# A router's weights scaled by the norm's row, its logits laid out by tokens, and a gather cut in four

## The chip, the cores and the metric

One core of one Trainium2 chip runs the program. The metric is device time in microseconds of one execution; the time before is the median of three runs. The trace is of one further, profiled execution.

## The reference, cut to what matters

Two blocks follow each other (256 tokens, width 1024, fp32). The first (mixer, cross attention, convolutional FFN, conformer) and the attention of the second are not touched. The change lies at the end, between the second block's last projection and its mixture of experts:

```python
x = x + mix @ w_out                        # the last projection, 1024 -> 1024
h = rmsnorm(x, g_ffn)                      # x * rsqrt(mean(x*x) + eps) * g_ffn
g_logits = h @ w_group + b_group           # 4 groups
e_logits = h @ w_router + b_router         # 4 x 8 experts; the best group's 8 are kept
e_w, e_idx = top_k(softmax(e_logits of that group), 2)
for e in range(32):                        # D_EXPERT = 512
    a = silu(h @ w_e_gate[e]) * (h @ w_e_up[e])
    out = out + gates[:, e:e+1] * (a @ w_e_down[e])
# then x + out goes through the final rmsnorm
```

## The kernel before

Tokens lie in two tiles t of 128 rows, `self.x[:, t]`; the width is cut into eight chunks of 128 (KC). Instructions are written in program order and a scheduler orders them on each engine; every engine then takes its queue strictly in that order. `self.after` adds an ordering without a semaphore.

**Last projection** (`proj_rows`, L293). The weights come as four loads of 1 MB; each is split on ScalarE into a rounded high part and on VectorE into the remainder (`split`, L202: L219, L220) in tiles named `whl`, of which there are four. The first two loads go through `proj_tm`; for the last two, four quarters b = (t, h) of the result, h being half the width, are finished one after the other (L315 to L317). After quarter b, `Norm.a` (L60) adds it to x (L67), multiplies by the norm's row into `xn` (L73) and squares on ScalarE; `Norm.b` (L87) transposes a quarter of `xn` on TensorE and copies it to `xnT`; `then` issues the router's logits.

**Router** (`moe`, L1128). The logits come out as 36 x 128 (L1170: weights `wr` stationary, `xnT` moving), are copied to `lt` and transposed back to tokens by 36 (L1186). `stats` makes rstd. L1191 applies rstd and bias; `first_max` and its neighbours, all on VectorE, choose experts; a small product with a triangle of ones (L1213) counts positions. `wr` is loaded on ScalarE's queue (L1155).

**Experts.** 32 experts go in 8 groups q of four, 32 token slots each. `gather` (L1230) makes `xq` (the chosen tokens, by chunks) with a one-hot matrix; for q = 0 in two halves of four chunks, before any expert product. `stream` (L1322) multiplies one chunk with four experts' weights; G, U and Y are gate, up and down. `acc` holds x plus the experts' output: four products with the identity put x there (L1275).

**Weights.** The experts' 201 MB are loaded on SyncE's queue (SP) in fixed order into 22 places of 1 MB (`wl`, L1314): five double buffers of their own (`pairs`, L1297), then places that earlier stages give up, in this order: one of its own, the three of the ring (free when VectorE has split the load in them), the four `whl` tiles (free when the projection's last product has read them), the two row tiles, `mh`, `ml`, and last the tile of x itself (free when the four products of L1275 have read it). The 23rd load reuses the first double buffer, and so waits for the first two chunks of G. SP issues in order: a load whose place is not free holds back all behind it.

Of the kernel before, what the change touches and what calls it, by code (L numbers as in the profile page):

```python
# [43 lines left out]
class Norm:  # L44
# [57 lines left out]
    def stats(self, t):  # L102
# [3 lines left out]
        nc.vector.scalar_tensor_tensor(r, ss[:, t, 0:1], EPS, ss[:, t, 1:2], op0=OP.add, op1=OP.add)  # L106
# [30 lines left out]
    def rcb(self, n):  # L137
        return self.rc[:, None, :].to_broadcast([P, n, T])


class Kern:
# [134 lines left out]
    def proj_tm(self, acc, w, ah, al, first):  # L276


        nc = self.nc
        wh, wl = self.split(self.wload(w, 2, D))  # L280
        for k in range(2):
            for t in range(2):
                sh = ah(k)[:, t * P:(t + 1) * P]
                sl = al(k)[:, t * P:(t + 1) * P]
                st = first and k == 0
                for h in range(2):
                    nc.tensor.matmul(acc[t][h], sh, wh(k)[:, h * 512:(h + 1) * 512], start=st, stop=False)  # L287
                for h in range(2):
                    nc.tensor.matmul(acc[t][h], sh, wl(k)[:, h * 512:(h + 1) * 512], start=False, stop=False)  # L289
                for h in range(2):  # L290
                    nc.tensor.matmul(acc[t][h], sl, wh(k)[:, h * 512:(h + 1) * 512], start=False, stop=False)

    def proj_rows(self, acc, w, ah, al, order, first=True, last=True, norm=None):  # L293
# [11 lines left out]
        for b in range(4):  # L305
            t, h = divmod(b, 2)
            ts_ = slice(t * P, (t + 1) * P)
            hs = slice(h * 512, (h + 1) * 512)
            for j, (i, wh, wl) in enumerate(ws):
# [818 lines left out]
    def moe(self, ctx, m, r2a):  # L1128
# [32 lines left out]
        lt = m1([36, 2, P], F32, "lt")  # L1161
        lps = []

        def logits(i):

            t, h = divmod(i, 2)
            if h == 0:
                lps.append(self.psr([36, P], "lp"))
            for k in range(4 * h, 4 * h + 4):
# [5 lines left out]
        norm = Norm(self, a["g_ffn_2"], then=logits,  # L1175
                    tiles=(lambda: m1([P, D], F32, "xn", f"xn{next(nX)}"), lambda: m1([P, 4, T], F32, "xnT", f"xs{next(nT)}")))
        self.proj_rows(self.acc4(), lambda i: a["w_out_2"][i], *m, range(4), norm=norm)
# [6 lines left out]
        lp = self.psr([P, 2, 36], "lp")  # L1184
        for t in range(2):
            tr = nc.tensor.transpose(lp[:, t], lt[:, t], self.ident[:36, :36])  # L1186
        Lg = m1([P, 2, 4], F32, "Lg")
        Le = m1([P, 2, 32], F32, "Le")
        for o, c0, c1 in ((Le, 4, 36), (Lg, 0, 4)):
            for t in range(2):  # L1190
                nc.vector.scalar_tensor_tensor(o[:, t], lp[:, t, c0:c1], norm.r[:, t:t + 1], rb[:, c0:c1], op0=OP.mult, op1=OP.add)  # L1191
# [38 lines left out]
        def gather(q, h, sel):  # L1230

            if h == 0:
                xq[q] = m1([P, KC, P], F32, "xq", f"xs{q % 2}")
            ps = self.psr([P, 4, P], "ga")
            for c in range(4):
                cs = slice((4 * h + c) * P, (4 * h + c + 1) * P)
                for t in range(2):
                    nc.tensor.matmul(ps[:, c], xn[t][:, cs], sel[:, t], start=(t == 0), stop=(t == 1))
            nc.scalar.activation(xq[q][:, 4 * h:4 * h + 4], ps, AF.Copy)

        sel = select(0)
        for h in range(2):
            gather(0, h, sel)
# [28 lines left out]
        acc = self.acc4()  # L1272
        for t in range(2):
            for h in range(2):
                nc.tensor.matmul(acc[t][h], self.ident, self.x[:, t, h * 512:(h + 1) * 512], start=True, stop=False)  # L1275
# [46 lines left out]
        def stream(ps, lh, q, i, st, en):  # L1322
            w = wl(q, i)
            for e in range(4):
                nc.tensor.matmul(ps[32 * e:32 * e + 32], lh[:, 32 * e:32 * e + 32], w(e), start=st, stop=en)  # L1325
# [39 lines left out]
        for q in range(NQ):  # L1365
            x_ = xq[q]
            G = self.psr([P, 512], "G")
            for k in range(KC):
                stream(G, x_[:, k], q, k, k == 0, k == KC - 1)
# [6 lines left out]
            for k in range(KC):  # L1376
# [6 lines left out]
                if k in (4, 6) and q + 1 < NQ:  # L1383
                    gather(q + 1, k // 2 - 2, sel)
# [220 lines left out]
```

## Time and profile before

| | |
|---|---|
| time, median of 3 runs | 1627.76 us (1627.6 to 1628.19) |
| the profiled execution: time / span | 1636.39 us / 1634.5 us |
| busy: TensorE, VectorE, ScalarE | 91%, 52%, 41% of the span |
| DMA in the last third (the experts) | busy throughout, 421 to 425 GB/s |

Times in rows are microseconds from the span's start. A row of the timeline has start, duration, engine, line, operation, result and operands, and in brackets the engine's idle time before it and what ended that. TensorE makes two passes for one fp32 product, so its counts are twice those of the code. "q" behind an engine's name is its sequencer, which issues DMAs. The page's 40 slices show TensorE at 90% and more until slice 31, and the DMA engines full from slice 29 to the last but one.

### The profile page before, as it was taken

To read this page: it belongs to the slowest core of one execution; us is meant where nothing else is said; L and a number is where in the kernel's file an instruction comes from. 1 tells how busy PE (TensorE), PEld (TensorE's weight loads), DVE (VectorE), ACT (ScalarE), POOL (GpSimd) and SP (SyncE) were. 2 spreads that over 40 slices of the span, in tenths; PEclk is the share of its full clock that TensorE was granted. 3 is DMA by queue.
4 is the path that set the end of the run, shared out by engine and by line. 5 is a ranking of instruction groups with operands and counts; after the bars stand their busy time and mean duration, and the time that the engine had idled before them with its cause. 6 is when DMAs were issued, how large, how long until landed. Compare 5 with 4: busy or idle time off the path is not lost. (4 is left out here: it accounts for less than half of the span.)

```text
span 1634.5 us, 23715 instructions
## 1 busy us (share of the span) xinstructions
PE 1479.8 (91%) x9724; PEld 1133.7 (69%) x9724; DVE 851.4 (52%) x1553; ACT 663.8 (41%) x1061; POOL 82.4 (5%) x146
## 2 busy tenths in 40 slices
PE   8999999999989999999999999999998777676665
PEld 7988889999987688999988789789643222221211
DVE  7975677666899566776676765765500000000000
ACT  5764555545676454545554444454311000000001
POOL 0000000000057000100000000000000000000000
PEclk9999999999999999999999999999989878897887
DMA  7555445555643443655545236247999999999996
GB/s 265 193 188 180 143 167 191 185 192 187 218 151 104 161 162 104 219 181 194 186 162 206 99 128 213 78 153 286 356 381 423 421 423 425 424 422 421 425 423 268
DMA packets 52049, 396.58 MB, mean 243 GB/s; under 512 B 5952, under 2 KB 6112, under 8 KB 12256
## 3 DMA queue, kind: packets, MB, share of 16 engines
q1 hardware_dynamic: 49824, 388.80, 62.0%
q0 software_dynamic: 1680, 5.79, 1.1%
q8 instruction: 78, 1.28, 0.3%
q10 hardware_dynamic: 432, 0.41, 0.1%
q14 instruction: 35, 0.29, 0.0%
HBM read 393.94 MB, written 1.05 MB: 242 GB/s over the span
## 5 line engine op out<-in xcount | busy, mean ns | idle before, releaser
L220 DVE TENSOR_TENSOR whl<-w,whl 128x1024 fp32r<-128x1024 f32 (+1 forms) x344 | 404.8, 1184 | 207.3 <-ACT whl L219 206.7
L219 ACT ACTIVATE whl<-w 128x1024 fp32r<-128x1024 f32 (+1 forms) x344 | 345.7, 1020 | 296.3 <-PE pr L270 147.0
L267 PE MATMUL pr<-xth,whl 128*128 128x256 f32 x1472 | 370.0, 283 | 0.0
L268 PE MATMUL pr<-xtl,whl 128*128 128x256 f32 x1472 | 366.8, 281 | 0.0
L267 PEld LDWEIGHTS pr<-xth,whl 128*128 128x128 f32 x1472 | 277.3, 188 | 3.7 <-issue 2.8
L268 PEld LDWEIGHTS pr<-xtl,whl 128*128 128x128 f32 x1472 | 277.2, 188 | 1.9 <-issue 1.1
L270 PE MATMUL pr<-xth,whl 128*128 128x256 f32 x1472 | 236.7, 281 | 1.2 <-DVE whl L220 1.2
L270 PEld LDWEIGHTS pr<-xth,whl 128*128 128x128 f32 x1472 | 200.4, 188 | 2.9 <-issue 1.5
L1387 DVE TENSOR_TENSOR as<-sg,tp 128x512 f32<-128x512 f32 x8 | 5.5, 687 | 241.1 <-ACT GUs L1330 117.2
L1325 PE MATMUL U<-w,xq 128*32 128x512 f32 x512 | 81.0, 719 | 37.4 <-DMA w<-in_w_e_dram 37.3
L1325 PE MATMUL Y<-w,as 128*32 128x512 f32 x512 | 77.4, 737 | 30.4 <-DMA w<-in_w_e_dram 25.4
L1325 PE MATMUL G<-w,xq 128*32 128x512 f32 x512 | 74.0, 671 | 32.5 <-DMA w<-in_w_e_dram 32.5
L1349 DVE COPY sct<-st 128x256 f32<-128x256 f32 x8 | 3.4, 424 | 160.9 <-PE st L1347 160.9
L1325 PEld LDWEIGHTS Y<-w,as 128*32 128x32 f32 x512 | 16.0, 126 | 84.0 <-DMA w<-in_w_e_dram 39.0
L1325 PEld LDWEIGHTS U<-w,xq 128*32 128x32 f32 x512 | 14.4, 119 | 84.0 <-DMA w<-in_w_e_dram 49.7
L1325 PEld LDWEIGHTS G<-w,xq 128*32 128x32 f32 x512 | 13.4, 116 | 83.3 <-DMA w<-in_w_e_dram 62.4
L1395 ACT ACTIVATE ys<-Y,sm 128x512 f32<-128x512 f32 x16 | 11.0, 687 | 130.0 <-PE Y L1325 130.0
L1330 ACT ACTIVATE GUs<-G,sm 128x512 f32<-128x512 f32 x8 | 5.5, 687 | 129.1 <-PE G L1325 129.1
L827 DVE SCALAR_TENSOR_TENSOR cps<-gl,vec,cps 128x252 f32<-128x252 f32 (+18 forms) x144 | 56.1, 468 | 1.7 <-ACT cps L797 1.6
L819 POOL TENSOR_TENSOR cv<-cv,prod 128x470 f32<-128x470 f32 (+9 forms) x40 | 50.4, 1263 | 18.8 <-ACT prod L815 16.3
L287 PE MATMUL pa<-whl,ah 128*128 128x512 f32 x160 | 49.4, 390 | 0.0
L289 PE MATMUL pa<-whl,ah 128*128 128x512 f32 x160 | 49.4, 390 | 0.0
(438 smaller groups left out, 2318.7 us busy)
## 6 DMA issues: line engine op xcount, KB each, us to landing
w<-in_w_e_dram SPq DMA_DIRECT2D x94, 1024.0 KB, 22.5
w<-in_w_e_dram SPq DMA_DIRECT2D x45, 2048.0 KB, 22.3
w<-in_f_w_up_dram SPq DMA_DIRECT2D x48, 1024.0 KB, 4.8
w<-in_w_in_dram SPq DMA_DIRECT2D x25, 1024.0 KB, 4.8
w<-in_f_w_down_dram SPq DMA_DIRECT2D x24, 1024.0 KB, 4.9
w<-in_c_w_pw_dram SPq DMA_DIRECT2D x12, 1024.0 KB, 4.9
w<-in_ab_w_in_dram SPq DMA_DIRECT2D x9, 1024.0 KB, 5.0
w<-in_xa_wk_dram SPq DMA_DIRECT2D x8, 1024.0 KB, 4.9
```

Source lines behind the costliest of these rows:

```text
L219: c = self.last_hi = nc.scalar.activation(h[:, s], src[:, s], AF.Copy)
L220: d = nc.vector.tensor_sub(l[:, s], src[:, s], h[:, s].bitcast(F32))
L267: nc.tensor.matmul(ps[:, j], wh(k)[:, js], xh(k), start=(k == 0), stop=False)
L268: nc.tensor.matmul(ps[:, j], wh(k)[:, js], xl(k), start=False, stop=False)
L270: nc.tensor.matmul(ps[:, j], wl(k)[:, js], xh(k), start=False, stop=(k == kc - 1))
L287: nc.tensor.matmul(acc[t][h], sh, wh(k)[:, h * 512:(h + 1) * 512], start=st, stop=False)
L289: nc.tensor.matmul(acc[t][h], sh, wl(k)[:, h * 512:(h + 1) * 512], start=False, stop=False)
L819: nc.gpsimd.tensor_add(y, y, pd)
L827: nc.vector.scalar_tensor_tensor(y, gl[g][:, j, :T - d], wc(d, 2 * g + j), y, op0=OP.mult, op1=OP.add)
L1325: nc.tensor.matmul(ps[32 * e:32 * e + 32], lh[:, 32 * e:32 * e + 32], w(e), start=st, stop=en)
L1330: nc.scalar.activation(s, src, AF.Copy, scale=gc[:, 1:2])
L1395: nc.scalar.activation(ys, Y, AF.Copy, scale=gc[:, 0:1])
```

## The change

The norm's row is multiplied into the router's weights (`wr`, by a new column tile `gcol` that a second small DMA on ScalarE's queue brings), so that x itself is transposed for the logits and `xn` is needed by the gather only. The logits come out as 128 x 36 directly. The last quarter of the projection is made in two pieces of 256 columns, each added, transposed and copied for itself. The gather for q = 0 goes in pieces of 1, 1, 2 and 4 chunks, with the products of chunks 0 and 1 of G between them. Three of the four products that put x into `acc` come behind the logits; the fourth comes behind chunk 3 of G.

```diff
+class RouterNorm(Norm):
+    def a(self, i, acc=None, sq=True):
...
+        if i < 3:
+            nc.vector.tensor_add(x, x, acc[t][h])
+            self.sq(i)
+            self.gain(i)
+    def gain(self, i):
+        t, h = divmod(i, 2)
+        hs = slice(h * 512, (h + 1) * 512)
+        return self.k.nc.vector.tensor_mul(self.xs[t][:, hs], self.k.x[:, t, hs], self.row[:, hs])
+    def piece(self, p, acc):
+        x = self.k.x[:, 1, 512 + 256 * p:768 + 256 * p]
+        self.k.nc.vector.tensor_add(x, x, acc[1][1][p])
+    def b(self, i):
...
+        k.transpose_half(k.x[:, t], t, h, self.th, None)
+        if i:
+            self.then(i - 1)
+    def last(self, p):
+        k, nc = self.k, self.k.nc
+        ps = k.psr([P, 2, P], "pt")
+        for c in range(2):
+            o = 512 + 256 * p + c * P
+            nc.tensor.transpose(ps[:, c], k.x[:, 1, o:o + P], k.ident)
+        return nc.vector.tensor_copy(self.ts[1][:, 2 * p:2 * p + 2, P:2 * P], ps)
@@ proj_rows
+            if b == 3 and isinstance(norm, RouterNorm):
+                norm.a(3)
+                for p in range(2):
+                    o = acc[1][1][p]
+                    cs = slice(512 + 256 * p, 768 + 256 * p)
+                    for j, (i, wh, wl) in enumerate(ws):
+                        for k in range(2):
+                            if (p, j, k) == (0, 1, 0):
+                                norm.b(2)
...
+                    norm.piece(p, acc)
+                break
@@ moe
-        lt = m1([36, 2, P], F32, "lt")
+        gcol = m1([P, KC], F32, "gcol")
+        nc.scalar.dma_start(gcol, a["g_ffn_c"])
+        nc.vector.tensor_tensor(wr, wr, gcol[:, :, None].to_broadcast([P, KC, 36]), op=OP.mult)
...
-                nc.tensor.matmul(lps[t], wr[:, k], norm.th(k)[:, t * P:(t + 1) * P], start=(k == 0), stop=(k == KC - 1))
-            if h == 1:
-                nc.scalar.activation(lt[:, t], lps[t], AF.Copy)
+                self.lp_last = nc.tensor.matmul(lps[t], norm.th(k)[:, t * P:(t + 1) * P], wr[:, k], start=(k == 0), stop=(k == KC - 1))
...
         logits(2)
-        norm.then = None
-        norm.b(3)
+        for p in range(2):
+            norm.last(p)
+        norm.sq(3)
         norm.stats(1)
-        logits(3)
+        for p in range(2):
+            logits(3, range(2 * p, 2 * p + 2))
+        acc = self.acc4()
+
+        def residual(t, h):
+            return nc.tensor.matmul(acc[t][h], self.ident, self.x[:, t, h * 512:(h + 1) * 512], start=True, stop=False)
+        for t, h in ((0, 0), (0, 1), (1, 0)):
+            self.after(self.lp_last, residual(t, h))
+        self.after(norm.stt, norm.gain(3))
...
-        for h in range(2):
-            gather(0, h, sel)
+        for c in range(2):
+            gather(0, c, 1, sel)
...
             for k in range(KC):
-                stream(G, x_[:, k], q, k, k == 0, k == KC - 1)
+                if q == 0 and k in (1, 2):
+                    gather(0, 4 * k - 4 or 2, 2 * k, sel)
+                mm = stream(G, x_[:, k], q, k, k == 0, k == KC - 1)
+                if q == 0 and k == 3:
+                    self.after(mm, residual(1, 1))
```

VectorE's queue where the last two loads of the projection are split (`whl` tiles from `w`), before and after. DMAHW in brackets is a DMA's semaphore, the others are engines'. Before:

```order
L332 TENSOR_TENSOR ml_11086<-gs_1228_9973,mh_11085 128x512 [waits Activation_49] x2
L220 TENSOR_TENSOR whl_11321<-w_11319,whl_11321 128x1024 [waits DMAHW0_49,Activation_49]
L1151 TENSOR_SCALAR tri_11237<-jp 128x128 [waits DVE_49]
L220 TENSOR_TENSOR whl_11324<-w_11319,whl_11324 128x1024 [waits Activation_49]
L220 TENSOR_TENSOR whl_11329<-w_11327,whl_11329 128x1024 [waits DMAHW1_49,Activation_49]
L220 TENSOR_TENSOR whl_11332<-w_11327,whl_11332 128x1024 [waits Activation_49]
L67 TENSOR_TENSOR x<-x,pa_11251 128x512 [waits PE_49]
```

The three splits behind `tri` follow each other there. After, from the same place on:

```order
L398 TENSOR_TENSOR ml_11086<-gs_1228_9973,mh_11085 128x512 [waits Activation_49] x2
L1217 TENSOR_SCALAR tri_11237<-jp 128x128 [waits DVE_49]
L265 TENSOR_TENSOR whl_11336<-w_11334,whl_11336 128x1024 [waits DMAHW0_49,Activation_49]
L1229 TENSOR_TENSOR wr_11241<-wr_11241,gcol_11246 128x288 [waits DMAHW4_49,DMAHW3_49]
L265 TENSOR_TENSOR whl_11339<-w_11334,whl_11339 128x1024 [waits Activation_49]
L265 TENSOR_TENSOR whl_11344<-w_11342,whl_11344 128x1024 [waits DMAHW1_49,Activation_49]
L265 TENSOR_TENSOR whl_11347<-w_11342,whl_11347 128x1024 [waits Activation_49]
L154 TENSOR_TENSOR x<-x,pa_11253 128x512 [waits PE_49]
```

The product of `wr` and `gcol`, which waits for both their DMAs, stands ahead of the last three splits.

TensorE's queue from the first expert product on, before and after (the gather's `ga` comes from `xn`; G's operands are loaded weights `w` and `xq`). Before:

```order
L1238 MATMUL ga_11519<-sel_11506,xn_11401 128x128
L1325 MATMUL G_11561<-w_11562,xq_11508 32x512 [waits DMAHW4_49,Activation_49]
L1325 MATMUL G_11561<-w_11562,xq_11508 32x512 x7
L1325 MATMUL G_11561<-w_11572,xq_11508 32x512 [waits DMAHW7_49]
L1325 MATMUL G_11561<-w_11572,xq_11508 32x512 x7
```

The whole gather is done there before the first product. After, with rows of the gather left out:

```order
L1396 MATMUL G_11572<-w_11573,xq_11539 32x512 [waits DMAHW4_49,Activation_49]
L1396 MATMUL G_11572<-w_11573,xq_11539 32x512 x3
L1313 MATMUL ga_11579<-sel_11537,xn_11362 128x128 [waits PE_49]
...
L1396 MATMUL G_11572<-w_11573,xq_11539 32x512 [waits Activation_49]
L1396 MATMUL G_11572<-w_11573,xq_11539 32x512 x3
L1313 MATMUL ga_11589<-sel_11537,xn_11362 128x128 [waits PE_49]
...
L1396 MATMUL G_11572<-w_11599,xq_11539 32x512 [waits DMAHW7_49,Activation_49]
L1396 MATMUL G_11572<-w_11599,xq_11539 32x512 x7
L1257 MATMUL pa_11478<-x,ident 128x512
```

Gather pieces now stand between the chunks of G, and the last product that reads x behind its fourth chunk (before, all four stood ahead of the gather).

SP's queue at the end of the first round of places: the load into x's tile, then the first of the second round. Before:

```order
L1285 DMA w_11735<-in_w_e_dram 128x2048 [waits DMAHW6_49]
L1285 DMA w_11741<-in_w_e_dram 128x2048 [waits DMAHW7_49,PE_49,Activation_49]
L1297 DMA w_11749<-in_w_e_dram 128x4096 [waits DMAHW0_49,PE_49]
L1297 DMA w_11762<-in_w_e_dram 128x4096 [waits DMAHW1_49,PE_49]
L1297 DMA w_11774<-in_w_e_dram 128x4096 [waits DMAHW2_49,PE_49]
```

Each of the second round waits for TensorE there. After:

```order
L1356 DMA w_11763<-in_w_e_dram 128x2048 [waits DMAHW7_49]
L1356 DMA w_11769<-in_w_e_dram 128x2048 [waits DMAHW0_49,PE_49,Activation_49]
L1368 DMA w_11777<-in_w_e_dram 128x4096 [waits DMAHW1_49]
L1368 DMA w_11790<-in_w_e_dram 128x4096 [waits DMAHW2_49]
L1368 DMA w_11802<-in_w_e_dram 128x4096 [waits DMAHW3_49,PE_49]
```

The order of the loads is the same; the first two of the second round no longer wait for TensorE themselves, since the load into x's tile ahead of them already waits for a later product.

## Rows read from the trace of the kernel before

**Rows 1.** Stretches: each engine's busy time, granted clock, DMA share, GB/s.
```profile
1190.00:1196.00 6.00, 6.00 (x51) 3.25 (x50) 0.00 (x0) 0.60 (x1) 0.00 (x0) 0.92 0.41 130
...
1300.00:1600.00 300.00, 204.71 (x1216) 61.56 (x1218) 10.30 (x39) 21.50 (x33) 0.00 (x0) 0.84 1.01 424
```

**Rows 2.** Waits of SP, 1140 to 1196: total us, times, longest.
```profile
SPq L1297 <- PE G L1325: 13.6, 2, 12.3
...
SPq L1285 <- PE pa L1275: 4.3, 1, 4.3
```

**Rows 3.** Timeline of SP's issues: x's tile, then the second round.
```profile
1180.85 0.33 SPq L1285 DMA_DIRECT2D w<-in_w_e_dram  x1
```
```profile
1193.57 5.05 SPq L1297 DMA_DIRECT2D w<-in_w_e_dram  x3
```

**Rows 4.** Timeline of VectorE: the splits of the last two loads.
```profile
1151.28 1.23 DVE L220 TENSOR_TENSOR whl<-w,whl 128x1024 fp32r<-128x1024 f32 x1 [0.20 <-ACT whl L219]
1152.42 0.30 DVE L1151 TENSOR_SCALAR tri<-jp 128x128 bf16<-128x128 int32 x1
1154.03 1.22 DVE L220 TENSOR_TENSOR whl<-w,whl 128x1024 fp32r<-128x1024 f32 x1 [1.30 <-ACT whl L219]
...
1159.63 1.22 DVE L220 TENSOR_TENSOR whl<-w,whl 128x1024 fp32r<-128x1024 f32 x1 [1.58 <-ACT whl L219]
```

**Rows 5.** The issue of wr's load on ScalarE's queue (timeline).
```profile
1151.17 0.33 ACTq L1155 DMA_DIRECT2D wr<-in_w_rt_dram  x1
```

**Rows 6.** DMA view, issued 1151 to 1154 (first SP row: 1150.77): KB, us to landing.
```profile
w<-in_w_e_dram SPq DMA_DIRECT2D x1, 2048.0 KB, 17.6
...
wr<-in_w_rt_dram ACTq DMA_DIRECT2D x1, 144.0 KB, 12.8
```

**Rows 7.** DMA view, ScalarE's queue (q10) in 1154:1159, then 1159:1164: packets, MB, share.
```profile
q10 hardware_dynamic: 63, 0.07, 4.2%
```
```profile
q10 hardware_dynamic: 81, 0.07, 4.9%
```

**Rows 8.** DMA view, 0.5 to 4: a load shaped like gcol's, 128 x 8.
```profile
sm<-in_ab_norm_c_dram ACTq DMA_DIRECT2D x1, 4.0 KB, 3.1
```

**Rows 9.** Timeline of TensorE: first quarter's use of the splits, last quarter's end.
```profile
1159.27 0.39 PE L316 MATMUL pa<-whl,mh 128*128 128x512 f32 x1
...
1160.91 0.50 PE L316 MATMUL pa<-whl,mh 128*128 128x512 f32 x1
```
```profile
1173.38 0.40 PE L317 MATMUL pa<-whl,ml 128*128 128x512 f32 x1
1173.71 1.06 PE L1170 MATMUL lp<-xnT,wr 128*36 128x128 f32 x8
...
1176.37 1.13 PE L1275 MATMUL pa<-x,ident 128*128 128x512 f32 x2
```

**Rows 10.** Timeline of VectorE: logits with rstd and bias; the selection matrix.
```profile
1179.83 0.41 DVE L1191 SCALAR_TENSOR_TENSOR Le<-lp,rn,rb 128x32 f32<-128x32 f32 x2 [4.38 <-PE lp L1186]
```
```profile
1184.45 0.42 DVE L1224 TENSOR_TENSOR sel<-iot,pos 128x256 f32<-128x256 f32 x1
```

**Rows 11.** Timeline of TensorE: the gather for q = 0 and the first products.
```profile
1185.02 6.64 PE L1238 MATMUL ga<-sel,xn 128*128 128x128 f32 x32 [0.88 <-DVE cmi L1219]
1191.59 3.64 PE L1325 MATMUL G<-w,xq 128*32 128x512 f32 x32
```

**Rows 12.** Stretches, as in rows 1: the granted clock around the gather.
```profile
1182.00:1184.00 2.00, 0.37 (x10) 0.33 (x9) 1.93 (x16) 0.21 (x1) 0.00 (x0) 1.00 1.02 418
...
1186.00:1188.00 2.00, 2.00 (x11) 2.00 (x11) 0.07 (x1) 0.00 (x0) 0.00 (x0) 0.50 0.99 401
...
1190.00:1192.00 2.00, 2.00 (x15) 1.62 (x17) 0.00 (x0) 0.30 (x1) 0.00 (x0) 0.76 0.46 188
```

**Rows 13.** Timeline of TensorE: sixteen gather passes at full clock; thirty-two product passes later.
```profile
1204.90 2.05 PE L1238 MATMUL ga<-sel,xn 128*128 128x128 f32 x16
```
```profile
1605.25 6.37 PE L1325 MATMUL Y<-w,as 128*32 128x512 f32 x32 [0.83 <-DVE as L1387]
```

More of the change, by code (lines that the diff above doesn't have):

```diff
@@ L285, in proj_tm @@
                 st = first and k == 0
+                parts = []
                 for h in range(2):
-                    nc.tensor.matmul(acc[t][h], sh, wh(k)[:, h * 512:(h + 1) * 512], start=st, stop=False)
-                for h in range(2):
-                    nc.tensor.matmul(acc[t][h], sh, wl(k)[:, h * 512:(h + 1) * 512], start=False, stop=False)
-                for h in range(2):
-                    nc.tensor.matmul(acc[t][h], sl, wh(k)[:, h * 512:(h + 1) * 512], start=False, stop=False)
+                    if isinstance(acc[t][h], list):
+                        parts += [(o, slice(h * 512 + 256 * p, h * 512 + 256 * p + 256)) for p, o in enumerate(acc[t][h])]
+                    else:
+                        parts.append((acc[t][h], slice(h * 512, (h + 1) * 512)))
+                for o, cs in parts:
+                    nc.tensor.matmul(o, sh, wh(k)[:, cs], start=st, stop=False)
+                for o, cs in parts:
+                    nc.tensor.matmul(o, sh, wl(k)[:, cs], start=False, stop=False)
+                for o, cs in parts:
+                    nc.tensor.matmul(o, sl, wh(k)[:, cs], start=False, stop=False)
     def proj_rows(self, acc, w, ah, al, order, first=True, last=True, norm=None):
@@ L308, in proj_rows @@
             hs = slice(h * 512, (h + 1) * 512)
+            if b == 3 and isinstance(norm, RouterNorm):
[7 more added lines that the diff above has]
+                                norm.b(2)
+                            sh, sl = ah(2 * i + k)[:, ts_], al(2 * i + k)[:, ts_]
+                            nc.tensor.matmul(o, sh, wh(k)[:, cs], start=False, stop=False)
+                            nc.tensor.matmul(o, sh, wl(k)[:, cs], start=False, stop=False)
+                            nc.tensor.matmul(o, sl, wh(k)[:, cs], start=False, stop=(j == 1 and k == 1))
+                    norm.piece(p, acc)
+                break
             for j, (i, wh, wl) in enumerate(ws):
@@ L1174, in moe @@
         nX, nT = iter(range(2)), iter(range(2))
-        norm = Norm(self, a["g_ffn_2"], then=logits,
-                    tiles=(lambda: m1([P, D], F32, "xn", f"xn{next(nX)}"), lambda: m1([P, 4, T], F32, "xnT", f"xs{next(nT)}")))
-        self.proj_rows(self.acc4(), lambda i: a["w_out_2"][i], *m, range(4), norm=norm)
+        norm = RouterNorm(self, a["g_ffn_2"], then=logits,
+                          tiles=(lambda: m1([P, D], F32, "xn", f"xn{next(nX)}"), lambda: m1([P, 4, T], F32, "xnT", f"xs{next(nT)}")))
@@ L1324, in stream @@
             for e in range(4):
-                nc.tensor.matmul(ps[32 * e:32 * e + 32], lh[:, 32 * e:32 * e + 32], w(e), start=st, stop=en)
+                mm = nc.tensor.matmul(ps[32 * e:32 * e + 32], lh[:, 32 * e:32 * e + 32], w(e), start=st, stop=en)
+            return mm
         def turn(src, gc):
@@ L1383, in moe @@
                 if k in (4, 6) and q + 1 < NQ:
-                    gather(q + 1, k // 2 - 2, sel)
+                    gather(q + 1, 2 * k - 8, 4, sel)
             tU = turn(U, gc)
```

49 lines of the change are left out of this document (29 added, 20 removed).

## The prediction

> **What bounds the kernel now.** I read the stretches first. From 1300 to 1600 the DMA engines are busy throughout at 424 GB/s [rows 1]: the experts' weights stream, and TensorE waits for them. In such a stage work on the engines costs nothing; the end comes when the last load lands, plus a fixed tail. So I looked for stretches in which the DMA engines stand still once the stream has begun. There is one: from 1190 to 1196 their share is 0.41 [rows 1], that is 6.00 x 0.59 = 3.5 us lost. The waits of SP say why: its longest there, 12.3 us, is for the first products of G [rows 2]. The timeline of SP shows the load into x's tile issued at 1180.85 and the next, first of the second round, at 1193.57 [rows 3]. By then the queue has run dry. I call 1193.57 the **restart**: every load behind it follows without a gap, so the end moves as the restart moves, plus what has to be loaded after it that was loaded ahead of it before. This also caps any gain: 3.5 us, 0.2%, if the dry stretch vanished.
>
> The restart hangs on a chain: the projection's last quarter ends at about 1173.7 (its last product starts at 1173.38 [rows 9]), logits reach VectorE at 1179.83 [rows 10], the gather starts at 1185.02, G at 1191.59 [rows 11].
>
> **Part 1: the wait for wr and gcol.** The product of `wr` and `gcol` is put on VectorE ahead of the last three splits of the projection's weights, and waits for two DMAs. Before, nothing but the first logits waited for `wr`. Its load is issued at 1151.17 [rows 5] and lands 12.8 us later [rows 6], at 1164.0, because it shares the DMA engines with 2 MB loads, of which the last, issued at 1150.77, lands after 17.6 us, at 1168.4 [rows 6]. `gcol` is issued behind it on the same queue. VectorE is free for the product at 1152.7, after the first split and `tri` [rows 4], and then stands. Queued behind it are the splits that ran at 1154.03, 1156.83 and 1159.63 [rows 4], and TensorE waits for each.
>
> When does `gcol` land? Not before `wr`, 1164.0. At most: from 1168.4 on SP has nothing in flight, since its next load needs a ring place that the blocked splits hold; a load of gcol's shape took 3.1 us whole at the start [rows 8], so 1171.5. In between: ScalarE's queue moved 63 packets from 1154 to 1159 and 81 from 1159 to 1164, its 144 packets being wr's 128 and 16 completions [rows 7]; they took turns with the 2 MB loads. `gcol` has 144 more, small ones. At that pace they need until about 1173, but the 2 MB loads thin out from 1167 on and the rest then goes quickly. I take 1167.5, bounds 1164.0 and 1171.5.
>
> Two rules of the Trainium skill, "DMA: Bandwidth & Descriptors", speak against this price. Section "Anatomy of one DMA" has about 2 us plus bytes over 436 GB/s for one DMA: an estimate of 2.3 us for wr, no stall at all; the 12.8 us of rows 6 speak against it. Section "Queues, rings and completion order" says an engine drains a whole packet of some 9 to 17 descriptors before it turns to the next queue: gcol would go in one turn and land just behind wr; the ten microseconds over which wr's packets spread in rows 7 do not look so, unless a packet is a single descriptor.
>
> From 1167.5: the product on 128 x 288 takes 0.45 (0.42 for 128 x 256 [rows 10]), then three splits at 1.14 us each, the distance from the split at 1151.28 to the operation behind it [rows 4]: the last ends at 1171.4, and TensorE resumes at 1171.5. The product that needs it ran at 1160.91 [rows 9]. **+10.6 us** for all that follows on TensorE (7.1 to 14.6). Nothing covers it: the first split that is late is needed at 1159.27 [rows 9], and TensorE's queue behind is the projection itself.
>
> **Part 2: the clock after the wait.** TensorE stands from 1159.3 to about 1169 and in part to 1171.5. Around the router the rows show 0.37 us of work in 1182 to 1184, then a granted clock of 0.50 (1.2 GHz) in 1186 to 1188, and full clock (2.4 GHz) only late in 1190 to 1192, though the gather had filled the engine since 1185.02 [rows 11, 12]. A pass of a product takes 6.37/32 = 0.20 us in the slow stretch [rows 13] and 3.64/32 = 0.114 at full clock [rows 11]. Some 5 us at the lower clock lose 5 x (1 - 0.114/0.20) = 2.2 us. **+2.2 us** (0 to 3.5).
>
> **Part 3: the router.** From the quarter's end to the logits on VectorE it took 1179.8 - 1173.7 = 6.1 us, with two extra copies, the transposes back and products with x between. Now: four logit products, about 1.0 (eight passes took 1.06 [rows 9]); two transposes 0.3; two copies of 128 x 256, 0.42 each as in rows 10; the sum with eps and the power on GpSimd, about 1.0. Together 3.1. **-3.0 us.** The last quarter in 256-column pieces and the split products of the earlier chunks change no number of columns: +0.1.
>
> **Part 4: gather in pieces.** Before, gather start to restart was 1193.57 - 1185.02 = 8.55 us. Now x's load is what SP waits for, and x is free only behind chunk 3 of G. In order, gather passes at 6.64/32 = 0.21 us in the slow stretch [rows 11]: two chunks, eight passes, 1.65; chunk 0 of G, eight passes, 1.65; two chunks, 1.65; chunk 1, 1.35 with the clock rising; four chunks at full clock, 2.05 [rows 13]; chunks 2 and 3, 1.8; the product with x, 0.55 (half of 1.13 [rows 9]). Sum 10.7 (8.5 if all ran at full clock). **+2.1 us.**
>
> **Part 5: x's load changes sides.** It is issued at the restart now instead of 12.7 us ahead [rows 3]: 1.05 MB at 424 GB/s [rows 1], **+2.5 us**. The two double buffers behind it come free with it, so SP then has 5 MB at once. The queue is dry by then: four `whl` places, half a row place, `mh` and `ml`, 6.5 MB or some 16 us, are issued around the quarter's end, and the restart lies 19 us behind it.
>
> Hidden: the three products with x (before, SP's wait for them was 4.3 us [rows 2]) now run while VectorE chooses experts; the row's product behind the sum fits into GpSimd's time; the tail of the kernel is untouched.
>
> **Sum.** 10.6 + 2.2 - 3.0 + 0.1 + 2.1 + 2.5 = +14.5 us. The profiled execution, 1636.39 us (1.9 more than its span), would go to 1650.9. The median of the runs shown is 8.6 us lower; the difference holds for both: 1627.8 + 14.5 = **1642.3**.
>
> **The rivals.**
> *No stall, no change.* If wr and gcol landed by 1157, parts 1 and 2 fall away: -3.0 + 0.1 + 2.1 + 2.5 = +1.7, 1629.5. Point of decision: the last split must end by 1160.9, so 1160.9 - 3.9 = 1157.0. For it: only that the DMAs' moment may differ from execution to execution. Against: a landing 7 us later in the only trace. The first of the two rules above would give just this. I give it 8%.
> *Faster.* Without a stall, and with the gather and G at full clock, part 4 is -0.1 and the sum -0.5; if moreover x's tile came free early, so that part 5 fell away, -3.0 us: 1624.8, still within 0.2%. Only the whole dry stretch, -3.5 us, passes that mark. The place is x's tile, and the order on SP shows its load ahead of the second round. 2%, and 2% more for a small gain that counts as no change.
> *gcol lands with wr.* VectorE goes on at 1164.1: part 1 is 7.1 and the sum 11.0, 1638.8; without part 2, 1636.6. The second rule above would give this. 20%.
> *gcol takes as long behind wr as wr took*, some 10 us, to 1174: part 1 is 17, the sum 21, 1648.8. 9%.
>
> **How the numbers follow.** The forecast itself, gcol landing between 1165 and 1171.5 (1639.5 to 1646.5): 59%. With gcol beside wr, 20%; late gcol, 9%; no stall, 8%; a gain, 4%, half of it too small to count. Range 1636 to 1647.5: it takes in the first two. 0.2% is 3.3 us, about what a measurement of this kernel can tell from no change. Faster by more 2%, within it 10%, slower by more 88%.
>
> **What would show it.** Right: VectorE idle from about 1152.7 to 1167 at the product with gcol, its releaser a DMA; TensorE idle from 1159.3 for about ten microseconds, then a granted clock of 0.5; the DMA engines dry for some 10 us before the quarter's end and again for about 4 us before the restart; the load into x's tile issued at about 1205 with two double loads right behind it; logits on VectorE about 3 us after the quarter's end. Wrong: splits at their old times, or a second round that begins before x's load. The step I trust least is gcol's landing.

## The result, and the profile after

The changed kernel takes 1645.54 us (median of seven runs, 1640.2 to 1650.78) against 1628.19 for the kernel before beside it (seven runs, 1627.6 to 1636.56). The ratio, taken over all runs, is 1.0082 with an interval of 1.0058 to 1.0106: slower by 0.8%, or 13.4 us of 1628, and clear of noise. (The two medians lie 17.4 us apart; they depend on how many short and long executions each kernel happened to have.)

Executions of one kernel differ by up to 10 us, and much of that arises far ahead of the change: in nine traces of kernels whose code is the same up to there, the last projection begins anywhere from 1139.79 to 1148.19. So I compare traces from a common point: the **stretch** from the last projection's first product to the end of the span. Its first product is this row, in the trace of before and in that of after (start, duration, engine, line, operation):

```profile
1147.13 0.63 PE L287 MATMUL pa<-whl,mh 128*128 128x512 f32 x2
```
```profile
1143.36 0.63 PE L338 MATMUL pa<-whl,mh 128*128 128x512 f32 x2
```

Before, the span ends at 1634.5: the stretch is 487.4 us. After, it ends at 1643.8: 500.4 us. The change costs **13.0 us** there, and times of after are set beside those of before by adding 3.77 us.

VectorE after (timeline; in brackets the idle time ahead and what ended it). These rows answer to [rows 4] and [rows 10]:

```profile
1147.51 1.22 DVE L265 TENSOR_TENSOR whl<-w,whl 128x1024 fp32r<-128x1024 f32 x1
1165.33 0.46 DVE L1229 TENSOR_TENSOR wr<-wr,gcol 128x288 f32<-128x288 f32 x1 [16.60 <-DMA gcol<-in_g_ffn_c_dram]
1165.71 3.49 DVE L265 TENSOR_TENSOR whl<-w,whl 128x1024 fp32r<-128x1024 f32 x3
...
1184.59 0.45 DVE L1266 SCALAR_TENSOR_TENSOR Le<-lp,rn,rb 128x32 f32<-128x32 f32 x2 [0.24 <-issue]
```

The engine stands for 16.6 us in front of a product that takes 0.46, and the three splits queued behind it come out in one piece at 1165.71. What held them, in the DMA view (KB, us from issue to landing), against [rows 6]:

```profile
wr<-in_w_rt_dram ACTq DMA_DIRECT2D x1, 144.0 KB, 12.9
gcol<-in_g_ffn_c_dram ACTq DMA_DIRECT2D x1, 4.0 KB, 17.5
```

TensorE after (timeline), to be held against [rows 9] and [rows 11]:

```profile
1155.27 0.40 PE L381 MATMUL pa<-whl,mh 128*128 128x512 f32 x1
1166.98 0.80 PE L382 MATMUL pa<-whl,mh 128*128 128x512 f32 x1 [11.32 <-DVE whl L265]
...
1170.02 0.39 PE L382 MATMUL pa<-whl,mh 128*128 128x512 f32 x1
...
1181.66 0.98 PE L1240 MATMUL lp<-wr,xnT 128*128 128x36 f32 x8
...
1189.83 1.59 PE L1313 MATMUL ga<-sel,xn 128*128 128x128 f32 x8 [0.88 <-DVE cmi L1294]
...
1193.21 1.40 PE L1313 MATMUL ga<-sel,xn 128*128 128x128 f32 x8
1194.54 1.06 PE L1396 MATMUL G<-w,xq 128*32 128x512 f32 x8
1195.54 2.05 PE L1313 MATMUL ga<-sel,xn 128*128 128x128 f32 x16
```
```profile
1199.37 1.13 PE L1257 MATMUL pa<-x,ident 128*128 128x512 f32 x2
```

It waits 11.3 us for the second split, and its first product on the last split runs at 1170.02. That product stood at 1160.91 in [rows 9]. The projection ends at 1181.66, and x is read for the last time by a product that runs at 1199.37. SP's side, against [rows 2, 3]: its timeline, its waits in 1140 to 1220 (total, times, longest), and two of its waits before in the same window:

```profile
1200.57 0.33 SPq L1356 DMA_DIRECT2D w<-in_w_e_dram  x1
1200.94 0.91 SPq L1368 DMA_DIRECT2D w<-in_w_e_dram  x2
```
```profile
SPq L1356 <- DVE whl L265: 26.5, 3, 19.5
SPq L1356 <- PE pa L1257: 14.8, 1, 14.8
SPq L1356 <- PE pa L372: 11.9, 2, 11.6
```
```profile
SPq L1285 <- DVE whl L220: 14.4, 3, 5.2
...
SPq L1285 <- PE pa L317: 11.4, 4, 8.6
```

The longest wait for a split is 19.5 us, where it was 5.2; the longest for the projection's products, which free the `whl` tiles, is 11.6 and was 8.6; and the product that frees x's tile is waited for 14.8 us, in place of the 12.3 for G of [rows 2]. What this does to the stream is read from the stretches (each engine's busy time, granted clock, DMA share, GB/s):

```profile
1160.00:1168.00 8.00, 1.02 (x2) 0.83 (x3) 2.67 (x4) 0.00 (x0) 0.00 (x0) 0.50 0.44 175
1168.00:1170.00 2.00, 2.00 (x6) 1.54 (x5) 1.20 (x2) 0.00 (x0) 0.00 (x0) 0.53 0.86 270
1170.00:1172.00 2.00, 2.00 (x10) 1.61 (x9) 1.28 (x2) 0.59 (x2) 0.00 (x0) 1.00 1.01 422
1174.00:1182.00 8.00, 8.00 (x63) 7.50 (x62) 2.76 (x6) 2.82 (x7) 0.56 (x1) 1.00 0.06 9
...
1198.00:1202.00 4.00, 4.00 (x36) 2.02 (x32) 0.46 (x2) 0.22 (x1) 0.00 (x0) 1.00 0.33 98
1300.00:1600.00 300.00, 204.48 (x1222) 60.20 (x1218) 10.31 (x39) 21.87 (x34) 0.00 (x0) 0.86 1.01 423
```

Three dry places, around 1163 to 1168, 1174 to 1182 and 1198 to 1202, one behind each of these waits, where before had the one of [rows 1]. From 1300 on the stream runs at 423 GB/s, against 424 before. The first 100 us of the stretch in one row each, before first:

```profile
1147.13:1247.13 100.00, 94.52 (x622) 52.84 (x620) 24.40 (x78) 23.26 (x38) 3.14 (x8) 0.95 0.95 385
```
```profile
1143.36:1243.36 100.00, 84.48 (x584) 49.97 (x583) 25.30 (x82) 21.86 (x36) 3.52 (x8) 0.93 0.82 330
```

The rate falls from 385 to 330 GB/s: in 100 us that is 5.5 MB less, and 5.5 MB at 424 GB/s are 13.0 us, all that was lost. So this stage, in which the engines have time to spare, is measured by its bytes.

### The profile page after: what moved, and what is told of

Read it like the earlier page. It is cut to its first block, busy times and chain, and to the rows that moved or that the text cites. A ratio compares the mean times of both kernels' runs of the same rounds, so it can differ in the third digit from the quotient of the medians.

```text
span 1643.8 us, 23761 instructions
## 1 busy us (share of the span) xinstructions
PE 1470.3 (89%) x9746; PEld 1128.1 (69%) x9746; DVE 852.2 (52%) x1557; ACT 662.7 (40%) x1060; POOL 82.5 (5%) x146
## 5 line engine op out<-in xcount | busy, mean ns | idle before, releaser
L1396 PE MATMUL Y<-w,as 128*32 128x512 f32 x512 | 73.9, 704 | 36.9 <-DMA w<-in_w_e_dram 31.8
L1396 PE MATMUL G<-w,xq 128*32 128x512 f32 x512 | 79.5, 718 | 29.2 <-DMA w<-in_w_e_dram 29.2
L885 POOL TENSOR_TENSOR cv<-cv,prod 128x470 f32<-128x470 f32 (+9 forms) x40 | 50.3, 1261 | 18.3 <-ACT prod L881 15.7
```

Of the source, the lines that this page charges most:

```text
L885: nc.gpsimd.tensor_add(y, y, pd)
L1396: mm = nc.tensor.matmul(ps[32 * e:32 * e + 32], lh[:, 32 * e:32 * e + 32], w(e), start=st, stop=en)
```

## The experiments

Theory: the price is the wait for `gcol` ahead of the splits (part 1), less what the router gains, plus the late release of x's tile (parts 4 and 5). Rivals: the new forms of the work (256-column pieces, logits by tokens, the gather in four) are slow themselves; or the weight loads would have paused there in any case. Every stretch below is its trace's span less the start of the first `pa<-whl,mh` product of L287 or its counterpart; the edits are abridged.

**The scale of comparison.** The kernel before, unchanged, profiled again.

> The kernel before once more, profiled in another execution, to see whether the stretch by which the runs are compared (from the last projection's first product to the end, 487.4 us in the first profile of it) is the same when the whole time is not. Theory (executions differ ahead of that stretch alone): 487.4 us within 0.7, whatever the span. Rival (the stretch itself scatters): it differs by 2 us or more, and differences of that size between kernels say nothing.

Span 1633.7, first product at 1146.27: 487.4 us, as in the first profile of it. Both executions were of similar length, so this supports the scale but doesn't test it at the far end. Two pairs of runs below do: they share all edits behind the first product, which comes 9.7 and 13.7 us apart in them, and their stretches agree within 0.2 and 0.4 us. In every run below whose start is not changed, the interval of the ratio of whole times contains the difference of the stretches.

**The stall alone**, put into the kernel before:

```
+ gcol = m1([P, KC], F32, "gcol")
+ nc.scalar.dma_start(gcol, a["g_ffn_c"])
+ wr2 = <128x288 of a tile that is not in use yet>
+ nc.vector.tensor_tensor(wr2, wr, gcol[:, :, None].to_broadcast(...), op=OP.mult)
```

> The kernel before, with one thing of the change added: gcol is fetched behind wr on ScalarE's queue, and VectorE multiplies wr by it into a tile that nothing reads, at the place in VectorE's order where the change has its product. Everything behind it is the kernel before. Theory (the wait for gcol is the cost): VectorE idles 15 to 18 us ahead of the product, the last projection's splits come 11 to 13 us later, and the stretch from wr's issue to the end grows by nearly that: 1639 to 1643 us. Rival 1 (the new form is what is slow): within 3 us of the kernel before, 1626 to 1631. Rival 2 (the weight loads have slack that takes the wait): VectorE idles as said and the time grows by under 6 us.

1649.84 us (four runs), ratio 1.011 with an interval of 1.0073 to 1.0147; first product at 1146.41, span 1647.9, stretch 501.5: **+14.1 us**. VectorE and the loads in its trace:

```profile
1170.28 0.46 DVE L1164 TENSOR_TENSOR GUs<-wr,gcol 128x288 f32<-128x288 f32 x1 [15.75 <-DMA gcol<-in_g_ffn_c_dram]
```
```profile
wr<-in_w_rt_dram ACTq DMA_DIRECT2D x1, 144.0 KB, 14.5
gcol<-in_g_ffn_c_dram ACTq DMA_DIRECT2D x1, 4.0 KB, 19.3
```

One product that nothing reads costs more than the whole change. The stage is a little over the 11 to 13 us expected, the whole time well over the 1639 to 1643: both loads took 1.6 to 1.8 us longer here than in the changed kernel. The product came to stand one split later than in the change, with two splits behind it and not three, so it copies the stall closely but not to the row. The wait alone is enough for the loss, in the old forms of the work, and the weight loads had no slack that took it. Whether the new forms add to it is what the next runs show.

**The change without the stall**: `wr` and `gcol` fetched ahead into tiles of their own, first with their issues among the first loads of the program, then in its middle (there each issue is ordered behind a square of the norm ahead). The product of the two goes ahead with them.

```
+ def router_weights(self):
+     nc.scalar.dma_start(self.wr, ...); nc.scalar.dma_start(self.gcol, ...)
- nc.scalar.dma_start(wr, ...); nc.scalar.dma_start(gcol, ...)      # at the router
```

> The changed kernel, but the router's weights wr and the gain's columns gcol are fetched ahead of the phase into tiles of their own, so the product wr*gcol waits for no transfer. Theory (the cost is the product on VectorE, which is waiting for gcol's 4 KB behind 2 MB weight loads and holds the splits of the last projection back): VectorE's idle time of 16.6 us ahead of that product is gone, the first product of the last projection on the last split comes some 12.9 us earlier than in the changed kernel, and of the 13.1 us that the stretch from wr's issue to the end had grown nearly all falls away: what stays is -1.0 (quarter) - 3.3 (tail of the norm to the router's logits) + 2.2 (cut gather to x's last reading) + 2.5 (x's load and the weight pairs late) = +0.4 us, so 1627 to 1631 us, no change against before. Rival 1 (the new form of the work is slow by itself: 256-column pieces, logits by tokens, four gathers): the wait is gone and the time stays near the changed kernel's, 1640 to 1646. Rival 2 (the wait was covered by the weight loads' own pace): the stall is gone, SyncE's weight loads have the same dry stretches, and the time stays above 1638.

First product at 1153.54, span 1640.8: 487.3, **-0.1 us** against before. VectorE's splits run as in [rows 4], 1.5 to 1.6 us of idle ahead of each. The whole time, 1635.95 us with a ratio of 1.0021 (0.9999 to 1.0043), didn't show it, and the 1627 to 1631 expected was missed. The stall had only moved. The product now stands near the head of VectorE's queue, at the program's start (timeline, then SP's longest wait in 0 to 22):

```profile
8.27 0.46 DVE L1234 TENSOR_TENSOR wr<-wr,gcol 128x288 f32<-128x288 f32 x1 [7.39 <-DMA gcol<-in_g_ffn_c_dram]
```
```profile
SPq L236 <- DVE whl L265: 8.7, 1, 8.7
```

`gcol` lands 6.5 us after its issue among the first loads; VectorE waits 7.4 us for it, its first splits come later, and SP's thirteenth issue, which waits for one of the splits, goes out at 19.67 us instead of 15.15 (19.23 in the other run with this edit, 14.4 to 15.4 in the twelve without it). The large loads themselves were not held up: the first 1 MB of weights took 11.2 us to land, 11.3 before. The stretch began 6.4 us later than in the first trace of before.

> As the first run with weights fetched ahead, except that wr's and gcol's loads are issued on ScalarE in the middle of the program (behind the squares of the norm ahead of the second feed-forward block) and not among the first loads of the program, where they held the start up by about 6 us. Theory (the wait for the two loads ahead of the splits is all that the change costs net): the stretch from the last projection's first product to the end is that of the kernel before within 1 us, as in that run (487.3 against 487.4 us), and now the whole time is too: 1627 to 1630 us by the lower runs, within 0.2% of before. Rival (the loads cost the same wherever they go): 3 us or more slower than before.

Here the loads go out at about 646 us. First product at 1143.89, span 1631.0: 487.1, **-0.3 us**; 1632.7 us, ratio 0.9997 (0.9978 to 1.0015). The product runs at 662.6 and waits for nothing. The stall was the whole net loss: 500.4 against 487.1. It is a net figure: what the new forms gain and what the late release of x costs are both still in it. Its DMA view shows how cheap the two loads are there, where the DMA engines are a fifth busy (share 0.20 from 640 to 650):

```profile
wr<-in_w_rt_dram ACTq DMA_DIRECT2D x1, 144.0 KB, 2.1
gcol<-in_g_ffn_c_dram ACTq DMA_DIRECT2D x1, 4.0 KB, 1.9
```

**Late release of x alone**, put into the kernel before:

```
  for t in range(2):
      for h in range(2):
-         matmul(acc[t][h], self.ident, x[t, h], ...)
+         if (t, h) != (1, 1): matmul(acc[t][h], self.ident, x[t, h], ...)
...
+ if q == 0 and k == 3: self.after(mm, matmul(acc[1][1], self.ident, x[1, 1], ...))
```

> The kernel before, with only the fourth product that reads x moved behind the fourth chunk of the first gate projection G. Theory: x's load leaves SyncE only after that product, at about 10 us behind the first product of the gather, and the weight pairs right behind it, so the restart of the weight loads comes later by what x's load adds: +2 to +5 us, 1630 to 1633 us. Rival 1 (the pairs wait for G's products 8.55 us behind the gather's start in any case, and x's 0.5 MB goes out beside them): within 1.5 us of before. Rival 2 (x's load ahead of the pairs was itself taking their place in the DMA queues): faster by 1 to 3 us, since the load no longer runs ahead of the pairs.

1642.5 us (1630 to 1633 expected), ratio 1.0039 (1.0016 to 1.0062); first product at 1148.08, span 1641.8, stretch 493.7: **+6.3 us**, more than the 2 to 5 expected. SP's waits in 1170 to 1200 and its timeline:

```profile
SPq L1286 <- PE pa L1373: 19.9, 1, 19.9
```
```profile
1176.59 21.17 SPq L1286 DMA_DIRECT2D w<-in_w_e_dram  x3
1197.80 6.24 SPq L1298 DMA_DIRECT2D w<-in_w_e_dram  x5
```

The 19.9 us stand in place of the 12.3 of [rows 2]. The pairs start at 1197.80, 3.3 us later than in [rows 3] once the 0.95 us by which this execution runs late are taken off; the load into x's tile, 1 MB or 2.5 us, went out ahead of the dry stretch and now goes out behind it, together with the pairs: 5.8 of the 6.3 us. My expectation had counted that load and too little of the later start.

**Early release of x in the changed kernel**: on top of the two runs with weights fetched ahead, the fourth product with x goes behind the logits like the other three.

```
- for t, h in ((0, 0), (0, 1), (1, 0)):
+ for t, h in ((0, 0), (0, 1), (1, 0), (1, 1)):
      self.after(self.lp_last, residual(t, h))
...
- if q == 0 and k == 3:
-     self.after(mm, residual(1, 1))
```

> The kernel with the weights fetched ahead (as in the first run of this call), and the fourth of the products that read x moved from behind the fourth chunk of the first gate projection G to right behind the logits, with the other three. Theory (x's tile comes free only with that product, which holds x's load at the head of SyncE's queue and the weight pairs behind it): x's load is out before the pairs are free, as in the kernel before, and the restart of the weight loads falls to the wait for the products of G. With the cut gather (10.7 us from its first product to that point, against 8.55 before) and a start 4.3 us earlier, the restart comes 2 to 6 us earlier than before, of which at most the dry stretch of the DMA ahead of it, some 3.5 us, can be gained: 1624 to 1628 us, and 2 to 5 us under the first run of this call. Rival (x's late load costs nothing, since the pairs wait for G anyway): the same as the first run of this call within 1 us.

First product at 1159.26, span 1642.6: 483.3, **-4.1 us** against before; the whole time again hides it behind the start of the program (1635.92 us where 1624 to 1628 were expected; ratio 1.0009, 0.9987 to 1.0031).

> The run before this one in the call, with the fourth product that reads x moved right behind the logits, so that x's tile is free early. Theory: the stretch from the projection's first product to the end is 483.3 us as in the run with x freed early, 4 us under before, and without the delay at the program's start the whole time shows it: 1623 to 1625 us by the lower runs, 0.2 to 0.3% faster than before. Rival (what is gained there is given back by the end of the program, or it was one execution's luck): within 1 us of before.

First product at 1145.61, span 1629.3: 483.7, **-3.7 us**. SP in this trace, x's tile and then the second round:

```profile
1177.57 0.33 SPq L1362 DMA_DIRECT2D w<-in_w_e_dram  x1
1183.64 0.33 SPq L1374 DMA_DIRECT2D w<-in_w_e_dram  x1
```
```profile
1145.61:1245.61 100.00, 93.55 (x672) 52.65 (x670) 25.77 (x82) 23.15 (x38) 3.52 (x8) 0.98 0.97 397
```

The second round starts at 1183.64, in before's times (1.52 us on) 1185.16 rather than 1193.57, and 397 GB/s against 385 are 1.2 MB or 2.8 us more. The rest is less certain: over the next 300 us the stream ran at 425 GB/s against 423, worth up to 1.4 us, and it did so in the run without the early release too. The whole time, 1631.79 us, shows less: ratio 0.9992 (0.9974 to 1.0011), and none of its runs reached the 1623 to 1625 expected (the fastest took 1628.94). That interval can't tell the 3.7 us from nothing.

**The order of the two loads**, in the changed kernel:

```
+ gcol = m1([P, KC], F32, "gcol")
+ nc.scalar.dma_start(gcol, a["g_ffn_c"])
  wr = m1([P, KC, 36], F32, "wr")
  nc.scalar.dma_start(wr, ...)
```

> The changed kernel, with gcol's load issued ahead of wr's on ScalarE's queue instead of behind it; the product stays on VectorE. Theory (4 KB land as late as they do because their packets wait behind wr's on the same queue): the wait ahead of the product ends with wr's landing, some 13 us behind the issue, and not 17.5; VectorE idles 11 to 13 us instead of 16.6, and the stretch from the projection's first product to the end grows by 8 to 9.5 us against before instead of 13.1. Rival (each load has its own wait behind the 2 MB weight loads on SyncE's queue, whatever the order): the product starts at the same place within 1 us, and the stretch grows by 12 to 13 us.

First product at 1148.19, span 1648.8: 500.6, **+13.2 us**, ratio 1.0076 (1.0051 to 1.0101). The 8 to 9.5 us of my theory were missed:

```profile
wr<-in_w_rt_dram ACTq DMA_DIRECT2D x1, 144.0 KB, 17.8
gcol<-in_g_ffn_c_dram ACTq DMA_DIRECT2D x1, 4.0 KB, 12.4
```

The 4 KB take 12.4 us where the 144 KB took 12.9 in the same place, and the 144 KB take 17.8 where the 4 KB took 17.5. The order decides which lands late, as the theory had it, but the bytes, on which its saving rested, don't matter here: what is second lands second. The DMA view of 1160 to 1164 shows why (packets, MB, share; q1 is SP's queue, q0 GpSimd's, q10 ScalarE's):

```profile
q1 hardware_dynamic: 98, 1.34, 79.5%
q0 software_dynamic: 98, 0.31, 18.9%
q10 hardware_dynamic: 98, 0.02, 2.2%
```

The three queues take turns packet by packet, whatever a packet holds. Each of the two loads has 128 rows, one for each partition, and makes 144 packets ([rows 7]; 288 for both here), so each needs as many turns as the other. No run changed the number of rows, so that fewer rows would land sooner stays an inference.

**The product on GpSimd**, in the changed kernel:

```
- nc.vector.tensor_tensor(wr, wr, gcol[...], op=OP.mult)
+ nc.gpsimd.tensor_tensor(wr, wr, gcol[...], op=OP.mult)
```

> The changed kernel, with the product wr*gcol on GpSimd's queue (behind its loads of the router's biases and of g_final, ahead of the norm's power) and both loads where the change has them. Theory (the wait costs because it stands ahead of the last projection's splits on VectorE, not because the router's weights come late): the splits run through, the first dry stretch of the weight loads is gone. gcol still lands some 22 us behind the first product of the last projection, a GpSimd product of this size takes about 1 us (its 128x460 adds took 1.2), and TensorE's first logits pass, which comes 19.2 us behind that first product when nothing waits, waits 3 to 4 us for it. From the projection's first product to the end the time grows by 2 to 4 us against the kernel before instead of the changed kernel's 13.1. Rival (weights that are late hold the logits and with them everything behind, whoever multiplies): TensorE waits for the product by 10 us or more and the stretch still grows by 10 or more.

First product at 1139.79, span 1635.0: 495.2, **+7.8 us**; ratio 1.0035 (1.0015 to 1.0054). The splits run through, and the wait reappears at the first logits (timeline of GpSimd and of TensorE, then stretches):

```profile
1162.91 0.67 POOL L1229 TENSOR_TENSOR wr<-wr,gcol 128x288 f32<-128x288 f32 x1 [16.47 <-DMA gcol<-in_g_ffn_c_dram]
```
```profile
1163.63 1.92 PE L1240 MATMUL lp<-wr,xnT 128*128 128x36 f32 x8 [4.50 <-POOL wr L1229]
```
```profile
1163.50:1168.00 4.50, 4.37 (x14) 3.86 (x15) 0.00 (x0) 0.00 (x0) 0.60 (x2) 0.50 0.27 113
1168.00:1170.00 2.00, 2.00 (x20) 1.95 (x18) 1.38 (x2) 0.73 (x3) 0.00 (x0) 0.99 0.00 0
```

A wait of 4.5 us, not 3 to 4, and behind it a granted clock of 0.50 (1.2 GHz) for 4.5 us. From the first logits pass to `Le` it takes 11.4 us, against 9.3 in the first run with weights fetched ahead: 2.1 us for the clock. My expectation of 2 to 4 had left the clock out; 4.5 + 2.1 is most of the 7.8. (The rival's 10 us and more did not come.)

**Order and engine both changed, with x released early**, and then with the first gather whole as well:

> Three edits on the changed kernel: gcol's load ahead of wr's, the product on GpSimd, and the fourth product that reads x right behind the logits with the other three. Theory: wr lands some 17 us behind the projection's first product, GpSimd's product ends about 1 us later, ahead of the first logits pass at 19.2, so nothing waits; x's load and the weight pairs come early as in the run with weights fetched ahead and x freed early, whose stretch from the projection's first product to the end came out 4.0 us shorter than before. Here the start of the program is that of the kernel before, so the whole time shows it: 3 to 4.5 us under before, about 1624 to 1625 where before's faster runs take 1628. Rival (what was gained there came from the early loads): no gain over before.

First product at 1146.75, span 1638.3: 491.6, **+4.2 us**, ratio 1.002 (1.0003 to 1.0037). The expected gain didn't come: it rested on `wr` landing after 13 us, and with `gcol` ahead it landed after 18.3, so that the first logits waited 4.6 us. Against the GpSimd run above, where they waited 4.5, x's early release is worth 3.6 us, much as before.

```
- gather(0, c, 1, sel)
+ gather(0, 4 * c, 4, sel)
...
- if q == 0 and k in (1, 2): gather(0, 4 * k - 4 or 2, 2 * k, sel)
```

> The kernel of the run before this one in the call, with the first gather whole again (two halves of four chunks, G's products unbroken behind it), as in the kernel before. Theory (the cut gather moves no bytes earlier; the end is set by when the weight loads run dry): the weight pairs wait for G's third product, which comes later or earlier by the shape of the gather by 1 to 2 us, and since little of the dry stretch is left there, within 1 us of that run in the stretch from the projection's first product to the end. Rival (the gather in pieces is what brings the early restart): 1.5 to 3 us slower than that run.

First product at 1147.75, span 1638.8: 491.1, 0.5 us less than the run before it, with the same ratio of 1.002 (1.0005 to 1.0036).

**The fastest version**: weights fetched in the middle of the program, x released early, the first gather whole.

> The run before this one in the call, with the first gather whole again and G's products unbroken behind it. Theory (the time goes by the bytes that the weight loads get through, and once x's tile comes free early the cut of the gather moves almost none): within 1 us of that run. Rival (the cut gather is what brings the early restart): 1.5 to 3 us slower than it.

1630.34 us (twelve runs, 1624.74 to 1634.26) against 1635.22 for before beside it: ratio **0.9979** (0.9962 to 0.9996). First product at 1144.08, span 1627.5: 483.4, -4.0 us. So it beats the kernel before by 0.2%, barely clear of noise, and it is the best of several versions tried. The gather in four pieces brings nothing once x is free early (0.3 to 0.5 us against it in two pairs, too little to call); SP still gets its second round early, at 1183.53 (1186.58 in before's times).

## Why the prediction held, point by point

The forecast was 1642.3, from +14.5 us; the stretch grew by 13.0 and the ratio says 13.4. The median, 1645.54, is within the range too, but the executions are spread as said, and three of the seven lie above it. The mechanism held; that the sum came so close is in part luck, since its errors cancel. By the steps:

- **What bounds the kernel**: right. The kernels differ by what they load in the first 100 us of the stretch (385, 330, 397 GB/s in the rows above), and the cap is about right: with the dry stretch ahead of the restart gone, the gain was 3.7 to 4.1 us where at most 3.5 were reckoned. The dry stretch foreseen ahead of the quarter's end came as two; between them went the loads into the ring's places that the late splits had freed.
- **Part 1**: the mechanism, the engine and what queues behind were right; the size was 2.3 us short. `gcol` landed at 1165.3, in before's times 1169.1, for a forecast of 1167.5 (and bounds 1164.0 and 1171.5). The product on the last split came 12.9 us late for the forecast 10.6: 1.6 us from the landing, the rest because TensorE, at half clock, had not finished with the split before when the last one was ready.
- **Part 2**: oversized. The clock was 0.50 and 0.53 up to 1170 and 1.00 from then on, only some 3 us after TensorE resumed at 1166.98. Those 3 us lay under the splits, so that 0.7 of the 2.2 us was left, and that is in the 12.9 already. Parts 1 and 2 together were forecast at 12.8: a landing 1.6 us later than forecast and a clock back 1.5 us cheaper cancelled, and that was luck. I had priced the recovery by the gather's rows [rows 12], where it came later. Where the engine resumes with nothing else to wait for, as with the product on GpSimd, the term is real: 2.1 us.
- **Last quarter**: from that product to the first pass behind the projection it took 11.6 us for 12.8 before, where I had +0.1. The logits passes between are 0.6 us of that: each now has 36 columns and not 128, and eight of them take 0.81 us up to the product behind them instead of 0.99. This I had overlooked; the other 0.6 I did not trace.
- **Part 3**: from there to `Le` 2.9 us (1181.66 to 1184.59) for 6.1: -3.2, forecast -3.0.
- **Part 4**: from the gather's first product to x's load 10.74 us (1189.83 to 1200.57), forecast 10.7. Its pieces were less exact. The product with x takes 1.2 us up to the load's issue and not 0.55: I halved the 1.13 of [rows 9], which is one product in its two passes. The clock was back at full from 1194 on, so the second gather piece and chunk 1 of G took 2.3 us and not 3.0. These cancel, by luck again.
- **Part 5**: x's load stands at the head of the restart and the pairs come 0.37 us behind it, as said. Parts 4 and 5 together were +4.7; three pairs of runs undid the late release and kept the gather in pieces, and gave 3.4 to 3.9.
- **Sum by measured terms**: 12.9 - 1.2 - 3.2 + 2.2 + 2.5 = 13.2, against 13.0 measured; the 2.5 is still the estimate of part 5, the others are read from the trace.

Of the rivals, "no stall, no change" was built, and gave -0.3 us where its own sum was +1.7; "faster" was built too, and its condition, x's tile free early, was the right one. "gcol lands with wr" is excluded: it landed 5.0 us behind it (issued 0.37 us later, 4.6 us longer on its way). So is "as long behind wr as wr took": 5.0 us and not 10. The rule of the Trainium skill, "DMA: Bandwidth & Descriptors", section "Anatomy of one DMA" (about 2 us plus bytes over 436 GB/s), is a fit to loads issued from GpSimd, which the prediction did not say; these two are issued from ScalarE. By it they would take an estimated 2.3 and 2.0 us: that agrees with the 2.1 and 1.9 us in the middle of the program, and is 10.6 and 15.5 us short beside the 2 MB loads. Its section "Queues, rings and completion order" (a whole packet of some 9 to 17 descriptors to each turn) would have let 4 KB land just behind what they follow. 5.0 us lay between, and the equal packet counts of the run with the order changed fit the prediction's "unless a packet is a single descriptor".

## What to carry to other kernels

A small load is priced by what is in flight when it is issued and by what stands ahead of it in its queue, not by its bytes: 4 KB cost 1.9 us in one place and 17.5 in another. Before an operation that needs a fresh load is put on an engine, look at what stands behind it in that engine's queue; if the queue feeds the main stream, fetch the data at a quiet place earlier, and see where the operation itself ends up: moved to another engine or to the program's start, the wait came back there. Where the stream of weights sets the end, count bytes in a stage: whatever frees the destination of the next load earlier (here the last reader of x) counts there, and shorter work only as far as it does that.

## What the runs showed that was not expected

- Two loads of 4 and 144 KB exchange their landing times (12.4 and 17.8 us, against 17.5 and 12.9) when their order is exchanged, and the queues in flight beside them get the same number of packets in a given time.
- With the same two among the first loads of the program, it is again VectorE's wait for `gcol`, 7.4 us, that delays SP's thirteenth issue, by 4.5 us.
- After a wait of 11.3 us TensorE was back at full clock within 3 us, in the same program in which the gather, begun at 1189.83, ran at 0.50 up to about 1193.5; with the product on GpSimd, after a wait of 4.5 us, it ran logits passes and products at 0.50 for 4.5 us.
